# A hybrid state-space and DeltaNet trunk: branch products, gates and merge turned channel-major, and temporaries moved by 32 bytes

## The chip, the cores and the metric

The kernel runs on one core of a Trainium2 chip. The metric is the device time of one execution in microseconds (us), the median over the runs. The engines are named as in the profile: PE (TensorE, the matrix unit; PEld is its weight load), DVE (VectorE), ACT (ScalarE), POOL (GpSimd) and SP (SyncE, which issues the DMAs). A matmul multiplies a *stationary* operand of 128 x 128, loaded into the array, with a *moving* operand that streams through it. Sums are formed in PSUM, in banks of 128 partitions x 512 fp32 values; everything else lies in SBUF.

## The reference

256 tokens of width 1024 go through two layers. Each is a feed-forward half step, a mixer, and another half step. The mixer runs two branches on the same normalised input and merges them through two gates:

```python
for l in range(DEPTH):
    h = h + 0.5 * swiglu(rms_norm(h, ffn1_norm[l]), ffn1_w_in[l], ffn1_w_out[l])
    u = rms_norm(h, mix_norm[l])
    (z_s, xbc, dt_s, qkv, z_d, b_d, a_d, gate_s, gate_d) = jnp.split(u @ w_in[l], split_points, axis=-1)
    y_s = mamba2_branch(z_s, xbc, dt_s, ...)
    y_d = deltanet_branch(qkv, z_d, b_d, a_d, ...)
    merged = (jax.nn.sigmoid(gate_s) * (y_s @ ssm_w_branch[l])
              + jax.nn.sigmoid(gate_d) * (y_d @ dn_w_branch[l]))
    h = h + merged @ w_out[l]
    h = h + 0.5 * swiglu(rms_norm(h, ffn2_norm[l]), ffn2_w_in[l], ffn2_w_out[l])
return rms_norm(h, final_norm)
```

The change concerns `gate_s`, `gate_d`, the two branch products, the merge, and what feeds and follows them. The state-space branch is normalised in four groups: the last step of each group scales its result `yg` by `rsqrt(mean(yg*yg) + EPS)`.

## The kernel before

**Products.** Every large product is formed from two-part operands: a value x is split into xh (rounded to fp32r) and xl = x - xh, and a product is the three matmuls h·h, h·l and l·h. `mm3` (lines 208 to 211) holds the tokens stationary and moves 512 columns of weights; its result is token-major, 128 tokens x 512 channels in one bank. `mm3w` (213 to 216) holds weights stationary and moves 256 tokens; its result is channel-major, 128 channels x 256 tokens. In the profile the token-major products carry the names `t` (units of the input projection, the gates `tg` among them), `b` (branch products) and `o` (output products); channel-major ones are `fc` (feed-forward), `xs`, `kk`, `qq`, `vv`, `bc` and others. Rows of the profile name the split operands: `uTh`/`uTl` is the normalised input with channels on partitions, `bh`/`bl` the branch input, `mh`/`ml` the merged value, `whi`/`wlo` the weights.

**Weights.** They come in halves of 128 x 1024 through one DMA queue in the order in which they are used. ACT writes `whi` from a half (line 60) and DVE `wlo` (line 63), up to five halves ahead (`take`, `prep`, `load`).

**The mixer.** A table of unit names, `ORDER`, lists in which order the units of the mixer are written down. The tile scheduler makes from it one instruction stream for each engine; each engine runs its stream in order and waits on semaphores of the others. The merge is written with a raised priority. Units of interest:
- `xGi`: a piece of the state-space input of group G, `xs`, with its convolution `ca` on DVE.
- `DG`: the decay matrix `dc` of group G, among its steps a multiply `dc<-dc,cbt` over 128 x 2048 on DVE.
- `SG` and `TG`: first and second part of the state-space step of group G. `TG` ends with the group's norm: ACT sums squares into `sss` (`jk,sss<-yz`), DVE scales `sss` (line 71), POOL raises it to the power -1/2 (`srr`, line 119), and ACT scales two tiles of `yz` with it (`yz<-yz,srr`).
- `gSnp`: half p of gate S (0 for the state-space branch, 1 for DeltaNet), columns 512n. ACT applies tanh(x/2), and the merge forms (1 + tanh) times the branch result. (The factor one half is applied behind `w_out`, with the residual sum.)
- `o`, line 883: `dn_T(0)`, four transposes `oT` on PE, `og` on DVE, and the split of `og` into `bh` on ACT and `bl` on DVE: input of the first of four stages of the DeltaNet branch.
- `N`: the DeltaNet branch product (`dn_branch`, 929), four stages, and the product with its gate. It is followed by `y`, the first input of the state-space branch (`ss_T`, transposes `yT`).

After `ORDER` come the state-space branch (eight stages), the merge and the product with `w_out`. **Merge** (989 to 1003): for each 128 tokens and 512 channels, `mt` = (1 + gate) times branch, `tg` += `mt`, four transposes `mT` of 128 x 128 on PE, since `w_out` needs channels on partitions, then `mh` on ACT and `ml` on DVE.

**Pools.** `cpool`, `wpool` and `slots` hold lasting tiles. Behind them `s2` holds nine rotating temporaries of 128 x 512 (among them `bh`, `bl`, `og`, `mt`) and `sm` small ones. All tiles of `s2` begin at a multiple of 128 bytes of a partition. `uTh` and `uTl` begin 32 bytes behind one, `whi` and `wlo` at one.

Of the kernel before, what the change touches and what calls it, by code (L numbers as in the profile page):

```python
# [16 lines left out]
P = 128  # L17
# [19 lines left out]

ORDER = """
z20 s z10 z11 s z21 s M k1 k0 q1 k2 k3 K1 K0 q3 q0 K3 K2 v0 q2 I Q0 I Q3 I z30 v1 z31 Q2 v2 V0 I v3
V1 I V3 I Q1 V2 d0 R R R b3 R b2 b0 R b1 R d2 R x00 R d1 x01 R d3 R R P R g100 g101 D0 S0 x10 T0 D1  # L40
x11 g110 g111 S1 x20 T1 o x21 N D2 y S2 D3 x30 x31 T2 g000 g010 g001 S3 g011 T3
""".split()


# [1 line left out]
def trunk_kernel(ctx, tc, x, wst, wsm, norms, lpar, rpar, cst, out):  # L46
# [3 lines left out]
    cpool = ctx.enter_context(tc.tile_pool(name="cpool", bufs=1))  # L50
    wpool = ctx.enter_context(tc.tile_pool(name="wpool", bufs=1))
    slots = ctx.enter_context(tc.tile_pool(name="slots", bufs=1))
    s2 = ctx.enter_context(tc.tile_pool(name="s2", bufs=9))
    sm = ctx.enter_context(tc.tile_pool(name="sm", bufs=1))
    accp = ctx.enter_context(tc.tile_pool(name="accp", bufs=4, space=PSUM))
# [3 lines left out]
    def act(o, i, func=AF.Copy, **kw):  # L59
        return A.activation(out=o, in_=i, func=func, **kw)  # L60

    def tt(o, a, b, op):
        return V.tensor_tensor(out=o, in0=a, in1=b, op=op)  # L63

    def stt(o, a, s, b, op0, op1):
        return V.scalar_tensor_tensor(out=o, in0=a, scalar=s, in1=b, op0=op0, op1=op1)
# [6 lines left out]
    def f(ap):  # L73
        return ap.bitcast(F32)

    def tmp2(name):
        return s2.tile([P, 512], F32, tag="s2", name=name)

    def trb(name):
        return trp.tile([P, 512], F32, tag="tr", name=name)  # L80

    def accb(name):
        return accp.tile([P, 512], F32, tag="acc", name=name)
# [63 lines left out]
    LAST = cs[:, 6 * P : 7 * P]  # L147
    mhalf = cpool.tile([P, 1], F32, name="mhalf")
    V.memset(mhalf[:], -0.5)

    one = cpool.tile([1, P], F32, name="one")
    V.memset(one[:], 1.0)
# [57 lines left out]
        PE.matmul(ps, lh, rl, start=False, stop=False)  # L210
        PE.matmul(ps, ll, rh, start=False, stop=stop)  # L211

    def mm3w(ps, wh, wl, mh, ml, start, stop):
        PE.matmul(ps, wh, mh, start=start, stop=False)  # L214
        PE.matmul(ps, wh, ml, start=False, stop=False)  # L215
        PE.matmul(ps, wl, mh, start=False, stop=stop)  # L216

    def tok_chunk(ps, ks):

# [110 lines left out]
    def mixer(l, nxt):  # L330
# [20 lines left out]
        def tok_unit(key, part, done):  # L351

            if part != 1:
                open_[key] = [accb("t0"), accb("t1")]
            tok_chunk(open_[key], range(KT) if part is None else range(4 * part, 4 * part + 4))
            if part != 0:
                for t in range(2):
                    done(t, open_[key][t])
# [512 lines left out]

        tg = {}

        def gate(s_, n, part):
            if s_ not in tg:
                tg[s_] = slots.tile([P, 2, D], F32, tag=("sA", "sD")[s_], name="tg")
            v = tg[s_][:, :, n * 512 : (n + 1) * 512]
            tok_unit(("g", s_, n), part, lambda t, ps: act(v[:, t, :], ps[:], AF.Tanh, scale=0.5))


        brT = {}
# [26 lines left out]
                stt(ol[:, k], bank[:, k * S : (k + 1) * S], w, f(oh[:, k]), ALU.mult, ALU.subtract)  # L908
            brT[("s", j)] = (oh, ol)

        def branch(kind, n, mk, tail=1):
            ps = [[accb("b"), accb("b")] for _ in range(2)]
            held = {}

            def stat(k, t):
                oh, ol = held[k // 2]
                return oh[:, k % 2, t * P : (t + 1) * P], ol[:, k % 2, t * P : (t + 1) * P]

            made = 1
            for j0 in list(range(n - tail)) + [n - tail]:  # L920
                js = range(j0, j0 + (tail if j0 == n - tail else 1))
                while made < min(js[-1] + 2, n):
                    mk(made)
                    made += 1
                for j in js:
                    held[j] = brT.pop((kind, j))
                out_chunks(ps, stat, [2 * j + i for j in js for i in range(2)], 2 * n - 1, group=2 * len(js))
            return ps

        def dn_branch():  # L930
            ps = branch("d", 4, dn_T)
            m = tg[1]
            for t in range(2):
                for n in range(2):
                    sl = slice(n * 512, (n + 1) * 512)
                    stt(m[:, t, sl], m[:, t, sl], 1.0, ps[t][n][:], ALU.add, ALU.mult)

        sc, inv, rc = scalars(), invert(), recur()
        units = {"k": k_unit, "q": q_unit, "v": v_unit}
# [42 lines left out]

        for name in ORDER:
            step(name)
        m = tg[1]
        ps = branch("s", 8, ss_T)
        mh = slots.tile([P, KT, S], F32R, tag="sE", name="mh")
        ml = slots.tile([P, KT, S], F32R, tag="sH", name="ml")
        def merge(t):
            for n in range(2):  # L990
                sl = slice(n * 512, (n + 1) * 512)
                mt = tmp2("mt")
                stt(mt[:], tg[0][:, t, sl], 1.0, ps[t][n][:], ALU.add, ALU.mult)
                tt(m[:, t, sl], m[:, t, sl], mt[:], ALU.add)
                bank = trb("mT")
                for k in range(4):
                    PE.transpose(bank[:, k * P : (k + 1) * P], m[:, t, n * 512 + k * P : n * 512 + (k + 1) * P], ident)
                oh = mh[:, 4 * n : 4 * n + 4, t * P : (t + 1) * P]
                ol = ml[:, 4 * n : 4 * n + 4, t * P : (t + 1) * P]
                bv = bank[:].rearrange("p (k t) -> p k t", k=4)  # L1000
                act(oh, bv)
                tt(ol, bv, f(oh), ALU.subtract)

        for t in range(2):
            with tc.high_priority(offset=PRI):
                merge(t)
        po = [[accb("o"), accb("o")] for _ in range(2)]

        def stat(k, t):
# [23 lines left out]
def _layout(inp):  # L1033
# [21 lines left out]
    for l in range(DEPTH):  # L1055
        def ffn(wi, wo):
            gate, up = wi[:, :FF], wi[:, FF:]
            wst.append(cols(np.concatenate([gate[:, :256], up[:, :256]], axis=1)))
            both = np.stack([gate[:, 256:].reshape(D, -1, P), up[:, 256:].reshape(D, -1, P)], axis=2)
            wst.append(chans(both.reshape(D, -1)))  # L1060
            wst.append(rows(wo))

        ffn(inp["ffn1_w_in"][l], inp["ffn1_w_out"][l])
        w = inp["w_in"][l]
        o = 0
        parts = []
        for s in (2048, 3072, 32, 3072, 1024, 8, 8, 1024, 1024):
            parts.append(w[:, o : o + s])
            o += s
        z_s, xbc, dt_s, qkv, z_d, b_d, a_d, g_s, g_d = parts  # L1070
        zs, kc, qc, vc = cols(z_s), chans(qkv[:, 1024:2048]), chans(qkv[:, :1024]), chans(qkv[:, 2048:])
        xc, zd, gs, gd = chans(xbc[:, :2048]), chans(z_d), cols(g_s), cols(g_d)
        pieces = {"N": rows(inp["dn_w_branch"][l])}
        pieces.update({f"z{g}{i}": zs[2 * g + i : 2 * g + i + 1] for g in range(GS) for i in range(2)})
        for key, w, n in (("k", kc, 4), ("q", qc, 4), ("v", vc, 4), ("d", zd, 4), ("b", chans(xbc[:, 2048:]), 4)):
            pieces.update({f"{key}{i}": w[i : i + 1] for i in range(n)})
        pieces.update({f"x{g}{i}": xc[2 * g + i : 2 * g + i + 1] for g in range(GS) for i in range(2)})
        for s, w in enumerate((gs, gd)):
            pieces.update({f"g{s}{n}{i}": w[2 * n + i : 2 * n + i + 1] for n in range(2) for i in range(2)})
        wst += [zs[:2]] + [pieces[name] for name in ORDER if name in pieces]  # L1080
        wst.append(rows(inp["ssm_w_branch"][l]))
        wst.append(rows(inp["w_out"][l]))
        ffn(inp["ffn2_w_in"][l], inp["ffn2_w_out"][l])
        wsm.append(np.concatenate([dt_s, a_d, b_d], axis=1).reshape(KT, P, 48).transpose(1, 0, 2))
        cw = np.zeros((48, P, 5), f32)
        dc = inp["dn_conv_w"][l]
        sc = inp["ssm_conv_w"][l]
        sb = inp["ssm_conv_b"][l]
        order = [(dc, 1024, 8, None), (dc, 0, 8, None), (dc, 2048, 8, None), (sc, 2048, 8, sb), (sc, 0, 16, sb)]
        i = 0  # L1090
        for cwt, c0, n, bias in order:
            for j in range(n):
                sl = slice(c0 + j * P, c0 + (j + 1) * P)
                cw[i, :, :4] = cwt[:, sl].T
                if bias is not None:
                    cw[i, :, 4] = bias[sl]
                i += 1
        lpar.append(
            np.concatenate(
                [cw.transpose(1, 0, 2).reshape(P, 240), inp["ssm_norm"][l].reshape(16, P).T, inp["dn_norm"][l].reshape(P, 1)],  # L1100
                axis=1,
            )
        )
        rpar.append(
            np.concatenate(
                [inp["ssm_dt_bias"][l], inp["dn_dt_bias"][l], inp["ssm_a_log"][l], inp["dn_a_log"][l], inp["ssm_d"][l]]
            )
        )
        norms += [inp["ffn1_norm"][l], inp["mix_norm"][l], inp["ffn2_norm"][l]]
# [40 lines left out]
```

## Time and profile before

| | us |
|---|---|
| median of three runs | 1596.07 |
| lowest and highest run | 1594.54 and 1596.31 |
| the profiled execution | 1593.43 |
| its span in the profile | 1591.6 |
| PE busy in the span | 1572.3 |
| DVE busy | 1069.1 |
| ACT busy | 880.1 |
| POOL busy | 58.1 |

Rows of the timeline give the start of an instruction and its duration, both in us, the engine, the line, the operation and its tile (out<-in), the shapes and a count. In square brackets stands how long the engine was idle before it, and what ended that. Rows of groups end with the busy time in us, the mean in ns of one instruction, and the idle time before them. Rows of windows give the stretch, its length, the busy time with the number of instructions that it touches, the granted TensorE clock (1.00 is full), the DMA share and GB/s. Matmuls overlap in the array: the listed duration of one is longer than the distance from its start to that of the next.

### The profile page before, as it was taken

Reading aid. Unit: us, or ns where it says so; the run is one execution under the profiler, and the core shown is the slowest. Engines: PE = TensorE matmul, PEld = TensorE weight load, DVE = VectorE, ACT = ScalarE, POOL = GpSimd, SP = SyncE. Lnnn points to the kernel's source line nnn. Section 1 sums busy time; section 2 is a strip of 40 time slices with the busy share of each in tenths; the row PEclk is TensorE's granted clock in tenths of the full one; section 3 lists DMA queues with packets and bytes.
Section 4 is the critical chain, followed back from the end, with each engine's and each line's share of the span. In section 5 each row is a group of like instructions: output and inputs, shape, how many; then the busy total and the mean of one; then the engine's idle time right before and its main releaser. Section 6 shows DMA issues by size and latency. Waiting matters only on the chain.

```text
span 1591.6 us, 28859 instructions
## 1 busy us (share of the span) xinstructions
PE 1572.3 (99%) x11672; PEld 1420.9 (89%) x11672; DVE 1069.1 (67%) x1550; ACT 880.1 (55%) x1416; POOL 58.1 (4%) x60
## 2 busy tenths in 40 slices
PE   8999999999999999999999999999999999999998
PEld 7999879999888888999899987899998888889986
DVE  5555468957899766555465555698579996675554
ACT  5444468756565654444354444686656665454443
POOL 0000020000000000000000001000000000000000
PEclk9999999999999999999999999999999999999999
DMA  7555465543465456555565565655436555555562
GB/s 268 193 188 195 161 203 192 166 149 117 173 214 172 159 170 189 188 192 190 173 207 190 186 196 174 197 176 180 129 120 207 178 170 175 172 175 194 187 196 96
DMA packets 91915, 284.73 MB, mean 179 GB/s; under 512 B 22069, under 2 KB 23045, under 8 KB 90758
## 3 DMA queue, kind: packets, MB, share of 16 engines
q1 hardware_dynamic: 91782, 282.90, 54.8%
q8 instruction: 91, 1.49, 0.4%
q14 instruction: 42, 0.34, 0.1%
HBM read 280.94 MB, written 1.92 MB: 178 GB/s over the span
## 4 chain that ended last, share of the span: by engine, by line
PE 91%; DVE 4%; DMA 2%; ACT 1%; POOL 1%; issue 0%; SPq 0%; POOLq 0%; ACTq 0%
PE fc L216 9%; PE fc L214 9%; PE fc L215 9%; PE o L211 6%; PE o L209 5%; PE o L210 5%; PE t L209 4%; PE t L210 3%; PE t L211 3%; PE b L211 3%; PE b L210 2%; PE b L209 2%; PE xs L215 2%; PE xs L214 2%; PE xs L216 2%; DVE wlo L63 1%
## 5 line engine op out<-in xcount | busy, mean ns | idle before, releaser
L63 DVE TENSOR_TENSOR wlo<-wraw,whi 128x1024 fp32r<-128x1024 f32 x504 | 613.6, 1223 | 376.4 <-ACT whi L60 369.3
L60 ACT ACTIVATE whi<-wraw 128x1024 fp32r<-128x1024 f32 x504 | 531.0, 1060 | 429.3 <-PE fc L215 176.2
L214 PE MATMUL fc<-uTh,whi 128*128 128x256 f32 x1280 | 357.4, 279 | 0.0
L215 PE MATMUL fc<-uTl,whi 128*128 128x256 f32 x1280 | 357.0, 279 | 0.0
L216 PE MATMUL fc<-uTh,wlo 128*128 128x256 f32 x1280 | 357.0, 279 | 0.0
L215 PEld LDWEIGHTS fc<-uTl,whi 128*128 128x128 f32 x1280 | 240.6, 188 | 0.2
L214 PEld LDWEIGHTS fc<-uTh,whi 128*128 128x128 f32 x1280 | 240.6, 188 | 0.2
L216 PEld LDWEIGHTS fc<-uTh,wlo 128*128 128x128 f32 x1280 | 240.6, 188 | 0.0
L209 PE MATMUL o<-whi,gh 128*128 128x512 f32 x352 | 137.3, 390 | 0.0
L210 PE MATMUL o<-wlo,gh 128*128 128x512 f32 x352 | 137.3, 390 | 0.0
L211 PE MATMUL o<-whi,gl 128*128 128x512 f32 x352 | 137.0, 389 | 0.0
L209 PE MATMUL t<-whi,uTh 128*128 128x512 f32 x256 | 103.2, 404 | 1.0 <-ACT uTh L60 1.0
L210 PE MATMUL t<-wlo,uTh 128*128 128x512 f32 x256 | 101.6, 397 | 0.0
L211 PE MATMUL t<-whi,uTl 128*128 128x512 f32 x256 | 101.1, 396 | 0.0
L211 PEld LDWEIGHTS o<-whi,gl 128*128 128x128 f32 x352 | 66.1, 188 | 13.8
L210 PEld LDWEIGHTS o<-wlo,gh 128*128 128x128 f32 x352 | 66.1, 188 | 13.6
L209 PEld LDWEIGHTS o<-whi,gh 128*128 128x128 f32 x352 | 66.1, 188 | 13.4
L209 PE MATMUL b<-whi,bh 128*128 128x512 f32 x192 | 76.3, 399 | 0.0
L210 PE MATMUL b<-wlo,bh 128*128 128x512 f32 x192 | 74.9, 390 | 0.0
L211 PE MATMUL b<-whi,bl 128*128 128x512 f32 x192 | 74.3, 394 | 0.6 <-DVE bl L63 0.6
L214 PE MATMUL xs<-uTh,whi 128*128 128x256 f32 x256 | 73.1, 286 | 0.0
L216 PE MATMUL xs<-uTh,wlo 128*128 128x256 f32 x256 | 71.6, 280 | 0.0
(259 smaller groups left out, 2915.6 us busy)
## 6 DMA issues: line engine op xcount, KB each, us to landing
wraw<-in_wst_dram SPq DMA_DIRECT2D x504, 512.0 KB, 4.3
dc<-rdram SPq DMA_DIRECT2D x8, 1024.0 KB, 9.2
nw<-in_norms_dram SPq DMA_DIRECT2D x6, 512.0 KB, 4.9
gb<-rdram SPq DMA_DIRECT2D x8, 256.0 KB, 6.1
h<-in_x_dram SPq DMA_DIRECT2D x4, 256.0 KB, 3.1
out_dram<-fo SPq DMA_DIRECT2D x4, 256.0 KB, 2.3
dq<-X SPq DMA_DIRECT2D x2, 256.0 KB, 4.8
cs<-in_cst_dram SPq DMA_DIRECT2D x1, 384.0 KB, 8.2
```

The source lines that it names most:

```text
L60: return A.activation(out=o, in_=i, func=func, **kw)
L63: return V.tensor_tensor(out=o, in0=a, in1=b, op=op)
L209: PE.matmul(ps, lh, rh, start=start, stop=False)
L210: PE.matmul(ps, lh, rl, start=False, stop=False)
L211: PE.matmul(ps, ll, rh, start=False, stop=stop)
L214: PE.matmul(ps, wh, mh, start=start, stop=False)
L215: PE.matmul(ps, wh, ml, start=False, stop=False)
L216: PE.matmul(ps, wl, mh, start=False, stop=stop)
```

## The change

Three parts:
1. Gates and branch products are formed channel-major: weights stationary, 256 tokens moving. A gate unit is now two channel groups of 128 in one bank, so four units `gS0` to `gS3` per gate in place of two pairs. In a branch each of the four banks holds two channel groups and takes its products stage by stage. The gate weights come in another layout, cut by channels.
2. The merge works on these channel-major tiles: gate, sum, `mh`, `ml`, without transposes and without the temporary `mt`.
3. A new pool `shift` with a tile of 32 bytes stands ahead of `s2` and `sm`, so that all their tiles begin 32 bytes behind a multiple of 128. POOL sets that tile to zero once.

```diff
-x11 g110 g111 S1 x20 T1 o x21 N D2 y S2 D3 x30 x31 T2 g000 g010 g001 S3 g011 T3
+x11 g12 g13 S1 x20 T1 o x21 N D2 y S2 D3 x30 x31 T2 g00 g01 g02 S3 g03 T3
...
+    shift = ctx.enter_context(tc.tile_pool(name="shift", bufs=1))
     s2 = ctx.enter_context(tc.tile_pool(name="s2", bufs=9))
     sm = ctx.enter_context(tc.tile_pool(name="sm", bufs=1))
...
+    gap = shift.tile([P, 8], F32, name="gap")
+    G.memset(gap[:], 0.0)
...
-        def gate(s_, n, part):
+        def gate(s_, u):
+
             if s_ not in tg:
-                tg[s_] = slots.tile([P, 2, D], F32, tag=("sA", "sD")[s_], name="tg")
-            v = tg[s_][:, :, n * 512 : (n + 1) * 512]
-            tok_unit(("g", s_, n), part, lambda t, ps: act(v[:, t, :], ps[:], AF.Tanh, scale=0.5))
+                tg[s_] = slots.tile([P, KT, S], F32, tag=("sA", "sD")[s_], name="tg")
+            ps = accb("g")
+            chan_chunk(ps)
+            act(tg[s_][:, 2 * u : 2 * u + 2, :].rearrange("p k t -> p (k t)"), ps[:], AF.Tanh, scale=0.5)
...
+        def branch(kind, n, mk):
+
+            ps = [accb("b") for _ in range(4)]
+            mk_at = 1
+            for j in range(n):
+                while mk_at < min(j + 2, n):
+                    mk(mk_at)
+                    mk_at += 1
+                oh, ol = brT.pop((kind, j))
+                ws = [take(), take()]
+                for b in range(4):
+                    for k, (wh, wl) in enumerate(ws):
+                        for a in range(2):
+                            c0 = (2 * b + a) * P
+                            mm3w(
+                                ps[b][:, a * S : (a + 1) * S], wh[:, c0 : c0 + P], wl[:, c0 : c0 + P],
+                                oh[:, k], ol[:, k], j == 0 and k == 0 and a == 0, j == n - 1 and k == 1, True,
+                            )
             return ps
+
+        def pair(v, b):
+
+            return v[:, 2 * b : 2 * b + 2, :].rearrange("p k t -> p (k t)")
...
-        def merge(t):
-            for n in range(2):
-                sl = slice(n * 512, (n + 1) * 512)
-                mt = tmp2("mt")
-                stt(mt[:], tg[0][:, t, sl], 1.0, ps[t][n][:], ALU.add, ALU.mult)
-                tt(m[:, t, sl], m[:, t, sl], mt[:], ALU.add)
-                bank = trb("mT")
-                for k in range(4):
-                    PE.transpose(bank[:, k * P : (k + 1) * P], m[:, t, n * 512 + k * P : n * 512 + (k + 1) * P], ident)
-                oh = mh[:, 4 * n : 4 * n + 4, t * P : (t + 1) * P]
-                ol = ml[:, 4 * n : 4 * n + 4, t * P : (t + 1) * P]
-                bv = bank[:].rearrange("p (k t) -> p k t", k=4)
-                act(oh, bv)
-                tt(ol, bv, f(oh), ALU.subtract)
+        with tc.high_priority(offset=PRI):
+            for b in range(4):
+                g, m = pair(tg[0], b), pair(tg[1], b)
+                stt(g, g, 1.0, ps[b][:], ALU.add, ALU.mult)
+                tt(m, m, g, ALU.add)
+                act(pair(mh, b), m)
+                tt(pair(ml, b), m, f(pair(mh, b)), ALU.subtract)
```

The scheduler makes other streams from this. Three places are of interest; the first two look the same in both layers. Line numbers of the changed kernel are shifted by a few.

ACT ahead of the DeltaNet branch `N` of the first layer, before: `jk,sss` are the sums of squares that end the second group's `T1`, `bh<-og` is the input of the first branch stage.

```order
L60 ACTIVATE jk,sss<-yz 128x512
L60 ACTIVATE whi<-wraw 128x1024
L60 ACTIVATE jk,sss<-yz 128x512
L60 ACTIVATE ca<-xs,lp 128x256
L60 ACTIVATE bh<-og 128x512
L60 ACTIVATE xsT<-ca 128x256
L60 ACTIVATE yz<-yz,srr 128x512 x2
L60 ACTIVATE whi<-wraw 128x1024
L60 ACTIVATE bh<-og 128x512
```

The same place in the changed kernel:

```order
L61 ACTIVATE jk,sss<-yz 128x512
L61 ACTIVATE whi<-wraw 128x1024
L61 ACTIVATE ca<-xs,lp 128x256
L61 ACTIVATE jk,sss<-yz 128x512
L61 ACTIVATE whi<-wraw 128x1024
L61 ACTIVATE xsT<-ca 128x256
L61 ACTIVATE yz<-yz,srr 128x512 x2
L61 ACTIVATE bh<-og 128x512 x2
```

The first `bh<-og` stood ahead of the pair `yz<-yz,srr` and stands behind it now, next to the second.

DVE at the start of the second part of group 1, `T1`, in the first layer, before: `xdt` and `xe` are inputs of its matmuls, `xD` the first result, and `sss` follows fifteen rows below the first row of `dc`.

```order
L63 TENSOR_TENSOR xe<-xdt,dE 128x512
L63 TENSOR_TENSOR wlo<-wraw,whi 128x1024
L70 TENSOR_SCALAR dc<-dc 128x2048
L66 SCALAR_TENSOR_TENSOR ca<-xs,lp,ca 128x255
L63 TENSOR_TENSOR xD<-xD,ydb 128x512
```

The same place in the changed kernel:

```order
L64 TENSOR_TENSOR xe<-xdt,dE 128x512
L64 TENSOR_TENSOR wlo<-wraw,whi 128x1024
L64 TENSOR_TENSOR dc<-dc,cbt 128x2048
L67 SCALAR_TENSOR_TENSOR ca<-xs,lp,ca 128x255
L64 TENSOR_TENSOR xD<-xD,ydb 128x512
```

The scaling `dc<-dc` of the third group has moved some eight rows up, and its multiply `dc<-dc,cbt`, which stood eleven rows behind `sss`, now stands ahead of it: of all instructions that DVE runs up to this `sss`, it is the only one more.

PE from the state-space branch to `w_out` of the first layer, before:

```order
L210 MATMUL b<-wlo,bh 128x512
L997 MATMUL mT<-cs,tg 128x128 x8
L211 MATMUL b<-whi,bl 128x512
L209 MATMUL b<-whi,bh 128x512
L210 MATMUL b<-wlo,bh 128x512
L211 MATMUL b<-whi,bl 128x512
L209 MATMUL o<-whi,mh 128x512
```

The same place in the changed kernel:

```order
L218 MATMUL b<-bh,whi 128x256
L219 MATMUL b<-bl,whi 128x256
L220 MATMUL b<-bh,wlo 128x256
L212 MATMUL o<-whi,mh 128x512
L213 MATMUL o<-wlo,mh 128x512
L212 MATMUL o<-whi,mh 128x512
L213 MATMUL o<-wlo,mh 128x512
L214 MATMUL o<-whi,ml 128x512
```

The transposes are gone (two more groups of four stood further on among the products of `w_out`), and `w_out` begins with four products that use `mh` alone.

More of the change, by code (lines that the diff above doesn't have):

```diff
@@ L39 @@
 z20 s z10 z11 s z21 s M k1 k0 q1 k2 k3 K1 K0 q3 q0 K3 K2 v0 q2 I Q0 I Q3 I z30 v1 z31 Q2 v2 V0 I v3
-V1 I V3 I Q1 V2 d0 R R R b3 R b2 b0 R b1 R d2 R x00 R d1 x01 R d3 R R P R g100 g101 D0 S0 x10 T0 D1
-x11 g110 g111 S1 x20 T1 o x21 N D2 y S2 D3 x30 x31 T2 g000 g010 g001 S3 g011 T3
+V1 I V3 I Q1 V2 d0 R R R b3 R b2 b0 R b1 R d2 R x00 R d1 x01 R d3 R R P R g10 g11 D0 S0 x10 T0 D1
+x11 g12 g13 S1 x20 T1 o x21 N D2 y S2 D3 x30 x31 T2 g00 g01 g02 S3 g03 T3
 """.split()
@@ L211, in mm3, with mm3w @@
         PE.matmul(ps, ll, rh, start=False, stop=stop)
[L213 to L216, printed above, removed]
+    def mm3w(ps, wh, wl, mh, ml, start, stop, shared=False):
+        PE.matmul(ps, wh, mh, start=start, stop=False, skip_group_check=shared)
+        PE.matmul(ps, wh, ml, start=False, stop=False, skip_group_check=shared)
+        PE.matmul(ps, wl, mh, start=False, stop=stop, skip_group_check=shared)
     def tok_chunk(ps, ks):
@@ L909, in ss_T @@
             brT[("s", j)] = (oh, ol)
[L911 to L927, printed above, removed]
-            return ps
+        def branch(kind, n, mk):
[15 more added lines that the diff above has]
+                            )
+            return ps
+        def pair(v, b):
+            return v[:, 2 * b : 2 * b + 2, :].rearrange("p k t -> p (k t)")
         def dn_branch():
             ps = branch("d", 4, dn_T)
-            m = tg[1]
-            for t in range(2):
-                for n in range(2):
-                    sl = slice(n * 512, (n + 1) * 512)
-                    stt(m[:, t, sl], m[:, t, sl], 1.0, ps[t][n][:], ALU.add, ALU.mult)
+            for b in range(4):
+                v = pair(tg[1], b)
+                stt(v, v, 1.0, ps[b][:], ALU.add, ALU.mult)
         sc, inv, rc = scalars(), invert(), recur()
@@ L984, in mixer @@
             step(name)
-        m = tg[1]
         ps = branch("s", 8, ss_T)
@@ L988, in mixer @@
         ml = slots.tile([P, KT, S], F32R, tag="sH", name="ml")
-        def merge(t):
-            for n in range(2):
-                sl = slice(n * 512, (n + 1) * 512)
-                mt = tmp2("mt")
-                stt(mt[:], tg[0][:, t, sl], 1.0, ps[t][n][:], ALU.add, ALU.mult)
-                tt(m[:, t, sl], m[:, t, sl], mt[:], ALU.add)
-                bank = trb("mT")
-                for k in range(4):
-                    PE.transpose(bank[:, k * P : (k + 1) * P], m[:, t, n * 512 + k * P : n * 512 + (k + 1) * P], ident)
-                oh = mh[:, 4 * n : 4 * n + 4, t * P : (t + 1) * P]
-                ol = ml[:, 4 * n : 4 * n + 4, t * P : (t + 1) * P]
-                bv = bank[:].rearrange("p (k t) -> p k t", k=4)
-                act(oh, bv)
-                tt(ol, bv, f(oh), ALU.subtract)
-        for t in range(2):
-            with tc.high_priority(offset=PRI):
-                merge(t)
+        with tc.high_priority(offset=PRI):
+            for b in range(4):
+                g, m = pair(tg[0], b), pair(tg[1], b)
[3 more added lines that the diff above has]
+                tt(pair(ml, b), m, f(pair(mh, b)), ALU.subtract)
         po = [[accb("o"), accb("o")] for _ in range(2)]
@@ L1071, in _layout @@
         zs, kc, qc, vc = cols(z_s), chans(qkv[:, 1024:2048]), chans(qkv[:, :1024]), chans(qkv[:, 2048:])
-        xc, zd, gs, gd = chans(xbc[:, :2048]), chans(z_d), cols(g_s), cols(g_d)
+        xc, zd, gs, gd = chans(xbc[:, :2048]), chans(z_d), chans(g_s), chans(g_d)
         pieces = {"N": rows(inp["dn_w_branch"][l])}
@@ L1078, in _layout @@
         for s, w in enumerate((gs, gd)):
-            pieces.update({f"g{s}{n}{i}": w[2 * n + i : 2 * n + i + 1] for n in range(2) for i in range(2)})
+            pieces.update({f"g{s}{i}": w[i : i + 1] for i in range(4)})
         wst += [zs[:2]] + [pieces[name] for name in ORDER if name in pieces]
```

## The prediction

> **What bounds the kernel now.** I read the page's busy times and clock first, then its chain of waits, then the groups by line, and last the timelines of the places that the change touches.
>
> ```profile
> span 1591.6 us, 28859 instructions
> PE 1572.3 (99%) x11672; PEld 1420.9 (89%) x11672; DVE 1069.1 (67%) x1550; ACT 880.1 (55%) x1416; POOL 58.1 (4%) x60
> PEclk9999999999999999999999999999999999999999
> PE 91%; DVE 4%; DMA 2%; ACT 1%; POOL 1%; issue 0%; SPq 0%; POOLq 0%; ACTq 0%
> L209 PE MATMUL b<-whi,bh 128*128 128x512 f32 x192 | 76.3, 399 | 0.0
> ```
>
> TensorE (PE) is busy for 99% of the span at full clock and carries 91% of the chain. So the change can win or lose only in the starts of PE: by the pitch of its matmuls, by matmuls that fall away, and by new waits. The last row counts the branch products: 192 of each of the three terms of a product, 576 matmuls in the program's two layers.
>
> **Pitch.** Matmuls overlap, so the price of one is the distance between starts, not its listed duration.
>
> ```profile
> 434.08 0.28 PE L214 MATMUL xs<-uTh,whi 128*128 128x256 f32 x1
> ...
> 438.98 0.28 PE L214 MATMUL xs<-uTh,whi 128*128 128x256 f32 x1
> 449.41 0.40 PE L209 MATMUL t<-whi,uTh 128*128 128x512 f32 x1
> ...
> 458.51 0.40 PE L209 MATMUL t<-whi,uTh 128*128 128x512 f32 x1
> 579.10 0.39 PE L209 MATMUL b<-whi,bh 128*128 128x512 f32 x1
> ...
> 586.58 0.39 PE L209 MATMUL b<-whi,bh 128*128 128x512 f32 x1
> ```
>
> 42 starts lie between the first two rows, 39 between the next, 33 between the last: 4.90/42 = 0.1167 us for 256 columns with a weight tile stationary, 9.10/39 = 0.2333 for 512 columns in the token-major units `t` (gates among them), 7.48/33 = 0.2267 in the branch `b`.
>
> Gates: each 512-column matmul becomes two of 256, 2 x 0.1167 = 0.2333. That is the old price, so 0. Each layer's eight tanh on ACT stay eight of 128x512.
>
> Branches: 576 x 0.2267 = 130.6 us become 1152 x 0.1167 = 134.4, **+3.8 us**. The nearest row, `xs`, is the same form as the new branch: weights stationary, and a moving tile (`uTh`) that already lies 32 bytes behind a multiple of 128, as `bh` will. What another placing of the moving tile would cost no row shows; the bound below is half of the old pitch, 0.1133, which gives 0. I take the row.
>
> The Trainium skill ("TensorE: Matmul & The Clock Gate", Back-to-back issue gap) gives an isolated matmul N/2.4 + 2.5 ns, 109 at 256 columns and 216 at 512; as an estimate by that page the term would be +1.5. Both of its figures lie under the pitches here (117 and 227), so the measurement decides.
>
> **The merge.** Before, 16 transposes `mT` per layer stand in the stream of PE.
>
> ```profile
> 586.81 0.39 PE L210 MATMUL b<-wlo,bh 128*128 128x512 f32 x1
> 587.04 1.21 PE L997 MATMUL mT<-cs,tg 128*128 128x128 f32 x8
> 588.01 0.48 PE L211 MATMUL b<-whi,bl 128*128 128x512 f32 x1
> ...
> 590.40 0.50 PE L211 MATMUL o<-whi,ml 128*128 128x512 f32 x1 [0.32 <-DVE ml L63]
> 586.81:593.94 7.13, 6.81 (x38) 1.00 0.44 144
> 590.86 0.68 DVE L66 SCALAR_TENSOR_TENSOR mt<-tg,b 128x512 f32<-128x512 f32 x1
> 591.46 0.68 DVE L63 TENSOR_TENSOR ml<-mT,mh 128x512 fp32r<-128x512 f32 x1
> ```
>
> The window from 586.81 to 593.94 touches 38 matmuls: one that is running at its start, one that begins at its end, 16 transposes and 20 products (4.53 us at 0.2267). The remaining 2.60 are the transposes, 0.97 for the first eight by the starts around them and so near 1.7 for all (two later groups of four cost 0.35 each in the same view), and some 0.9 of waits and restarts. All of it goes if the new seam does not wait. In the new branch the last stage works bank by bank, 12 matmuls each, so the four banks end 4.2, 2.8, 1.4 and 0 us ahead of the end of the branch, and merging begins while PE still multiplies. Per bank VectorE (DVE) does three instructions at 0.60 us pitch (590.86 to 591.46) and ACT one; behind the last two `wlo` of the branch I get bank 0's `mh` 0.75 us before and its `ml` 0.4 us after the branch's end. The first four products of `w_out` need `mh` alone (0.9 us). The last `ml` is there at +5.6, and the last quarter of 96 products at 0.2267 begins at +16. So nothing waits: 2 x 2.60 = **-5.2 us**. If the seam waited as long as before (0.9) it would be -3.3.
>
> **The new wait.** Two instructions are moved, both shown row by row ahead of this text. On DVE the `dc<-dc,cbt` of the third state-space group now stands ahead of the second group's rest, which ends in `sss`; on ACT the first `bh<-og` of the DeltaNet branch now stands behind the two `yz<-yz,srr`, which wait for POOL's power, which waits for `sss`. Before, that `bh` went first:
>
> ```profile
> 475.70 0.15 DVE L71 TENSOR_SCALAR sss<-sss 128x2 f32<-128x2 f32 x1
> 475.93 2.21 POOL L119 TENSOR_TENSOR srr<-sss,mhalf 128x2 f32<-128x2 f32 x1 [25.62 <-DVE sss L71]
> 475.76 0.62 ACT L60 ACTIVATE bh<-og 128x512 fp32r<-128x512 f32 x1
> 478.17 1.34 ACT L60 ACTIVATE yz<-yz,srr 128x512 f32<-128x512 f32 x2 [1.49 <-POOL srr L119]
> 479.41 1.05 ACT L60 ACTIVATE whi<-wraw 128x1024 fp32r<-128x1024 f32 x1
> 476.43:483.10 6.67, 6.37 (x25) 1.00 0.33 95
> 476.34 0.27 PE L902 MATMUL yT<-cs,yz 128*128 128x128 f32 x1
> 476.43 0.50 PE L209 MATMUL b<-whi,bh 128*128 128x512 f32 x1
> 482.76 0.50 PE L211 MATMUL b<-whi,bl 128*128 128x512 f32 x1 [0.30 <-DVE bl L63]
> 483.10 0.39 PE L209 MATMUL b<-whi,bh 128*128 128x512 f32 x1
> ```
>
> PE reached the branch at 476.43, the moment `bh` ended. In the new order it arrives there as early, and behind the branch's first matmul stands all of PE. When does `bh` end now?
>
> ```profile
> 445.88 2.28 DVE L63 TENSOR_TENSOR dc<-dc,cbt 128x2048 f32<-128x2048 f32 x1
> 448.08 0.47 DVE L66 SCALAR_TENSOR_TENSOR ca<-xs,lp,ca 128x255 f32<-128x255 f32 x1
> 441.10:475.70 34.60, 33.88 (x50) 1.00 0.67 222
> L119 POOL TENSOR_TENSOR srr<-sss,mhalf x8: 697/1604/2205, 448.7 to 1331.3; 128x2 f32<-128x2 f32 x8
> 482.02 0.68 DVE L63 TENSOR_TENSOR bl<-og,bh 128x512 fp32r<-128x512 f32 x1
> ```
>
> The moved multiply takes 448.08 - 445.88 = 2.20 us of DVE. The window shows DVE busy for 33.88 of 34.60 us ahead of `sss`, so at most 0.72 is absorbed: `sss` comes 1.5 to 2.2 late, at 477.2 to 477.9; I take 477.55. POOL starts 0.23 later (as 475.70 to 475.93) and takes 0.70 to 2.21, median 1.60: the end is 479.38. The two `yz` take 1.24 on ACT (478.17 to 479.41), `bh` 0.62: 481.27, the first product at 481.32. The new order lets three products pass before `bl`, which DVE has ready 0.68 later; PE runs freely from about 482.07. With the same work before (three half products, 0.35, and three transposes `yT` at the 0.09 between 476.34 and 476.43) the old kernel stood at 477.05: 5.02 late, with a restart of 0.11 (482.76 to 483.10 against 0.2267) 5.13. Against this stand the old kernel's own waits on the same stretch, which the new order of chunks lacks: the window of PE's branch products from 476.43 to 483.10 counts 25, so 24 pitches (5.44) and two `yT` (0.18) in 6.67 us, 1.05 of waits. Net 4.08, say **+4.1 us per layer**, +8.2 in two; the second layer's rows read alike. PE is the bound after it as before it, so no later slack gives it back.
>
> Bounds: with DVE not late at all and POOL's shortest 0.70 it is 4.1 - 1.85 - 0.90 = 1.35; with `sss` at 477.9 and 2.21 it is 5.1.
>
> **Small parts.** POOL's one memset runs at the start on an engine busy 58 us. ACT and DVE write tiles 32 bytes off at no price that a row shows:
>
> ```profile
> L63 DVE TENSOR_TENSOR uTl<-hnT,uTh 128x512 fp32r<-128x512 f32 x24 | 15.7, 686 | 5.8 <-ACT uTh L60 5.7
> L63 DVE TENSOR_TENSOR ml<-mT,mh 128x512 fp32r<-128x512 f32 x8 | 5.5, 684 | 0.1
> ```
>
> `uTl` lies at 32, `ml` at 0: 686 against 684 ns. As stationary operand a tile at 32 (`t`) costs 6.7 ns more than one at 0 (`b`); some 144 transposes of temporaries get such an operand, up to 1 us, much of it behind waits. I take 0.
>
> **Sum.** -5.2 + 3.8 + 8.2 = **+6.8 us**. The profiled execution took 1593.43 (its span 1591.6 and 1.8 around it), so 1600.2 is expected; the runs have a median of 1596.07, 2.6 more, and on that scale it is **1602.9**.
>
> **The rivals.**
> - *The chain is short* (not slower). DVE gives up idle time and `sss` comes no later, POOL's power takes its 0.70, and the wait is 1.35 per layer: -5.2 + 3.8 + 2.7 = +1.3, 1597.4. For it: POOL takes 0.70 in two of its eight, and what follows `sss` on DVE has changed. Against it: DVE's 0.72 of idle time. It decides from a wait under (3.2 + 1.4) / 2 = 2.3 per layer: `bl` ready before about 480.3.
> - *The wait lowers the clock.* PE would stand from about 476.8 to 481.3, 4.5 us. The longest PE wait inside the mixer is 1.6, with the granted clock at 1.00:
>
> ```profile
> PE cbb L778 <- DVE vb L63: 2.0, 2, 1.6
> 12.36 0.63 PE L209 MATMUL f<-whi,uTh 128*128 128x512 f32 x1
> 14.50 0.63 PE L211 MATMUL f<-whi,uTl 128*128 128x512 f32 x1
> ```
>
> At the program's start, behind idle time, five pitches take 2.14: 0.43 each instead of 0.2333. If each wait were followed by ten 512-column pitches of that kind, 2 us per layer are added: +10.8, 1606.9. No trace here holds a pause so long in mid-program. The Trainium skill (same page, HAM oscillation) states the rule: no PE gap over about 3.4 us, or the clock halves until the array has been busy again. With windows that run freely a pause of 4.5 need not cover one, so I hold it under an even chance.
> - *The aligned pitch.* If the new branch runs at 0.1133, its term is 0 and the sum +3.0: 1599.1, still slower through the wait.
> - *No late `bh`.* If ACT's order did not bind, -5.2 + 3.8 = -1.4, 1594.7. The rows `whi` behind `yz` at 479.41 show that ACT keeps its order, so this is slight.
>
> **Chances.** Forecast 0.57; clock 0.18; short chain 0.12; aligned pitch 0.08; no late `bh` 0.05. Under 0.2% (3.2 us) a measurement cannot tell this kernel from no change. The last case and the short chain give "same" and, with the aligned pitch, a little "faster": faster 0.06, same 0.18, slower 0.76. The range reaches from 1596.5 (a short chain with part of the cheaper pitch) to 1608 (wait at its upper bound, 1604.9, with part of the clock's loss).
>
> **What would show it.** The first `b` after the `oT` transposes should start about 4.7 us behind the last `yT`, with a wait on ACT's `bh`, in both layers; ACT should idle on `srr` with `bh` right behind; `sss` should stand 1.5 to 2.2 us later against PE; branch rows should have a pitch of 0.1167; from the branch's last matmul to `w_out`'s no pitch should exceed 0.25. I am wrong if `bh` is ready before PE, if the granted clock leaves 1.00, or if the seam waits for `mh`.

## The result, and the profile after

The changed kernel takes 1602.57 us, the median of four runs (1601.62 to 1603.47), beside 1595.3 for the kernel before in the same comparison: a ratio of 1.0048 with an interval of 1.0031 to 1.0066, so 4.9 to 10.5 us slower. Forecast were 1602.9 and 6.8 us more.

The page of the changed kernel, its busy times, the clock, and the branch's first term; then PE's waits (us in total, times, the longest):

```profile
span 1600.5 us, 30716 instructions
PE 1576.5 (99%) x12600; PEld 1469.0 (92%) x12600; DVE 1068.0 (67%) x1550; ACT 878.0 (55%) x1416; POOL 55.1 (3%) x61
PEclk9999999999999999999999999999999999999999
L218 PE MATMUL b<-bh,whi 128*128 128x256 f32 x384 | 108.7, 288 | 6.8 <-ACT bh L61 6.8
```

```profile
PE b L218 <- ACT bh L61: 6.8, 2, 3.4
```

PE is the bound as before, and one new row leads its waits: twice 3.4 us for the first `bh` of the DeltaNet branch, once in each layer. The page's slices of 40 us show no lower clock, since a fall of a few microseconds leaves each of them over nine tenths. The timeline of the place in the first layer, PE:

```profile
475.68 0.66 PE L908 MATMUL yT<-cs,yz 128*128 128x128 f32 x4
479.72 0.61 PE L218 MATMUL b<-bh,whi 128*128 128x256 f32 x3 [3.38 <-ACT bh L61]
480.45 0.39 PE L219 MATMUL b<-bl,whi 128*128 128x256 f32 x1
...
481.12 0.42 PE L220 MATMUL b<-bh,wlo 128*128 128x256 f32 x1
481.33 0.41 PE L218 MATMUL b<-bh,whi 128*128 128x256 f32 x1
481.55 0.41 PE L219 MATMUL b<-bl,whi 128*128 128x256 f32 x1
...
484.32 0.28 PE L218 MATMUL b<-bh,whi 128*128 128x256 f32 x1
484.43 0.28 PE L219 MATMUL b<-bl,whi 128*128 128x256 f32 x1
```

The windows of PE around it (stretch, length, busy, granted clock):

```profile
480.45:484.32 3.87, 3.87 (x20) 0.56 0.27 104
484.32:490.00 5.68, 5.68 (x50) 1.00 0.00 0
1270.45:1276.20 5.75, 5.75 (x26) 0.50 0.28 92
```

After the wait the clock is granted at 0.56 for 3.87 us: the products start 0.21 us apart (481.12, 481.33, 481.55) where 0.1167 is the pitch at full clock, from 484.32 on. The last row is the second layer, where PE starts again at 1270.45: there the clock is at half for 5.75 us. What PE waited for, on DVE, POOL and ACT:

```profile
475.95 0.15 DVE L72 TENSOR_SCALAR sss<-sss 128x2 f32<-128x2 f32 x1
476.01 1.21 DVE L64 TENSOR_TENSOR wlo<-wraw,whi 128x1024 fp32r<-128x1024 f32 x1
476.17 1.61 POOL L120 TENSOR_TENSOR srr<-sss,mhalf 128x2 f32<-128x2 f32 x1 [24.78 <-DVE sss L72]
477.81 1.33 ACT L61 ACTIVATE yz<-yz,srr 128x512 f32<-128x512 f32 x2 [1.03 <-POOL srr L120]
479.06 0.61 ACT L61 ACTIVATE bh<-og 128x512 fp32r<-128x512 f32 x1
```

The chain is the forecast one: `sss`, POOL's power, two scalings on ACT, and only then `bh`, whose end at 479.67 releases PE.

### The profile page after: what moved, and what is told of

It reads as the page before. It is cut to its first block, busy times and chain, and to the rows that moved or that the text cites. A ratio compares the mean times of both kernels' runs of the same rounds, so it can differ in the third digit from the quotient of the medians.

```text
span 1600.5 us, 30716 instructions
## 1 busy us (share of the span) xinstructions
PE 1576.5 (99%) x12600; PEld 1469.0 (92%) x12600; DVE 1068.0 (67%) x1550; ACT 878.0 (55%) x1416; POOL 55.1 (3%) x61
## 4 chain that ended last, share of the span: by engine, by line
PE 91%; DVE 4%; DMA 2%; ACT 1%; POOL 1%; issue 0%; SPq 0%; POOLq 0%; DVEq 0%; ACTq 0%
PE fc L218 9%; PE fc L219 9%; PE fc L220 9%; PE o L214 5%; PE o L212 5%; PE o L213 5%; PE b L219 3%; PE b L220 3%; PE b L218 3%; PE g L218 2%; PE g L220 2%; PE g L219 2%; PE t L212 2%; PE t L213 2%; PE t L214 2%; PE xs L218 1%
## 5 line engine op out<-in xcount | busy, mean ns | idle before, releaser
L218 PE MATMUL b<-bh,whi 128*128 128x256 f32 x384 | 108.7, 288 | 6.8 <-ACT bh L61 6.8
L219 PE MATMUL b<-bl,whi 128*128 128x256 f32 x384 | 109.2, 285 | 0.1
L220 PE MATMUL b<-bh,wlo 128*128 128x256 f32 x384 | 108.7, 284 | 0.0
L218 PEld LDWEIGHTS b<-bh,whi 128*128 128x128 f32 x384 | 73.3, 193 | 7.2 <-ACT bh L61 7.2
L219 PEld LDWEIGHTS b<-bl,whi 128*128 128x128 f32 x384 | 74.2, 193 | 0.3 <-DVE bl L64 0.3
L220 PEld LDWEIGHTS b<-bh,wlo 128*128 128x128 f32 x384 | 74.2, 193 | 0.0
L218 PE MATMUL g<-uTh,whi 128*128 128x256 f32 x256 | 73.0, 285 | 0.0
```

The source lines that it names most:

```text
L218: PE.matmul(ps, wh, mh, start=start, stop=False, skip_group_check=shared)
L219: PE.matmul(ps, wh, ml, start=False, stop=False, skip_group_check=shared)
L220: PE.matmul(ps, wl, mh, start=False, stop=stop, skip_group_check=shared)
```

## The experiments

All were timed in five rounds or more beside the kernel before. For the stages there is also a measure within one execution: the time from the start of PE's last `cbb` row to that of its last `o<-whi,mh` row in a layer, the mixer's second half. In both layers, in us:

| kernel | median | ratio to before, interval | second half, layer 1 and 2 |
|---|---|---|---|
| before | 1595.07 to 1595.52 | | 190.52, 190.55 |
| `after_again`, the change again | 1602.75 | 1.0049, 1.0035 to 1.0063 | 194.52, 194.88 |
| `o_early` | 1590.24 | 0.9968, 0.9955 to 0.998 | 189.03, 188.98 |
| `keepwarm` | 1600.23 | 1.0032, 1.002 to 1.0045 | 193.57, 193.58 |
| `noshift` | 1605.41 | 1.0059, 1.0046 to 1.0072 | 196.27, 196.28 |
| `before_gap` | 1598.32 | 1.0015, 1.0004 to 1.0026 | 193.93, 192.78 |
| `before_late` | 1601.44 | 1.003, 1.0019 to 1.0041 | 193.67, 193.97 |
| `cbt_back` | 1594.41 | 0.999, 0.998 to 1.0001 | 190.85, 190.55 |
| `cbt_back_late` | 1600.16 | 1.0026, 1.0017 to 1.0035 | 194.16, 193.22 |
| `x30_fill` | 1594.56 | 0.999, 0.9979 to 1.0 | 190.55, 190.38 |
| `o_early_cbt` | 1589.86 | 0.9963, 0.9949 to 0.9976 | 189.11, 189.09 |

### The change again, and `bh` early

> The changed kernel as it is, for a scale beside the others. Theory A (the late bh costs a wait of 3.4 us and the clock's fall behind it another 1.7 to 2 us per layer; pitch +3.8 and seam -5.2 in all): +7 us against before, TensorE waits for ACT's bh twice 3.4 us, and the granted clock is about 0.55 for 4 us behind each wait. Rival B (the clock's fall was an accident of one execution): +3 to +4 us, granted clock 1.00 there.

Measured: 7.7 us slower than before, and the wait and the low clock in both layers again. Theory A.

```diff
-x11 g12 g13 S1 x20 T1 o x21 N D2 y S2 D3 x30 x31 T2 g00 g01 g02 S3 g03 T3
+x11 g12 g13 S1 x20 o T1 x21 N D2 y S2 D3 x30 x31 T2 g00 g01 g02 S3 g03 T3
```

> The first DeltaNet branch input is written ahead of T1, so that its bh stands ahead of the two scalings of yz on ACT again; all else as in the change. Theory A: both waits and both falls of the clock go, at least 4.6 us per layer: 1.4 to 2 us faster than before the change (ratio about 0.999), 9 us faster than the changed kernel. Rival C (the wait only moves to the second branch stage, whose bh still stands behind the scalings): the wait of TensorE for bh comes back there with 2 us or more per layer, and the time is 1598 or more. Rival D (the loss lies in the 256-column branch itself): still 5 us or more slower than before.

Measured: 1590.24, 12.5 us faster than the change and 4.8 us faster than before (3.2 to 7.2 by the interval). The moved word `o` takes the whole unit with it, its four transposes, `og` and `bl` too. On ACT `bh` now ends nine microseconds ahead of the scalings, and PE passes from the transposes straight into the branch; the window covers the whole DeltaNet branch.

```profile
466.79 0.63 ACT L61 ACTIVATE bh<-og 128x512 fp32r<-128x512 f32 x1 [0.23 <-DVE og L67]
476.37 1.34 ACT L61 ACTIVATE yz<-yz,srr 128x512 f32<-128x512 f32 x2 [0.20 <-POOL srr L120]
477.61 0.62 ACT L61 ACTIVATE bh<-og 128x512 fp32r<-128x512 f32 x1
```

```profile
474.08 0.60 PE L893 MATMUL oT<-cs,vb 128*128 128x128 f32 x4
474.44 0.37 PE L218 MATMUL b<-bh,whi 128*128 128x256 f32 x1
```

```profile
474.44:497.72 23.28, 23.28 (x203) 1.00 0.53 166
```

PE is busy for 23.28 of 23.28 us at full clock, though the second `bh` still stands behind the scalings: it is ready (477.61 + 0.62) before its stage begins. Rivals C and D fall. What the change cost beyond its gains is the late `bh`, 5.5 to 5.9 us in each layer by the table. This kernel is faster than both.

### The clock's share

```diff
                 ws = [take(), take()]
+                if kind == "d" and j == 0:
+                    fill = trb("fill")
+                    for i in range(12):
+                        PE.matmul(fill[:], uTh[:, i % KT, :P], ws[0][0][:, :512], start=i == 0, stop=i == 11)
                 for b in range(4):
```

> The changed kernel with twelve unread 512-column products (2.8 us) on TensorE in each layer's pause ahead of the DeltaNet branch; the late bh stays. Theory A: TensorE begins the branch as late as in the changed kernel, but the granted clock stays 1.00: 3.4 to 4 us faster than the changed kernel in two layers, still 3 us slower than before. Rival B' (the slow pitch of 0.21 us has to do with the first products of the branch, its banks or its operands, not with the pause): no faster than the changed kernel, the slow rows stay.

```profile
474.50 3.04 PE L930 MATMUL fill<-whi,uTh 128*128 128x512 f32 x12
477.37 1.04 PE L893 MATMUL oT<-cs,vb 128*128 128x128 f32 x8
479.77 0.62 PE L218 MATMUL b<-bh,whi 128*128 128x256 f32 x3 [1.04 <-ACT bh L61]
480.50 0.39 PE L219 MATMUL b<-bl,whi 128*128 128x256 f32 x1
```

```profile
479.77:484.00 4.23, 4.23 (x34) 1.00 0.46 144
```

The branch begins as late as in the change (479.77 against 479.72) and with 12 idle products more, but the clock stays at 1.00, and the kernel is 2.5 us faster, 1.0 to 1.3 per layer by the table. That is theory A's direction and less than its 3.4 to 4. So the pause, not the first products, lowers the clock. By the change's own rows the slow stretch of the first layer holds 19 pitches in 3.87 us (480.45 to 484.32), 2.22 at full clock, so it costs 1.65 us. In `after_again` the clock is low from the first product of the branch on (0.50 from 479.18 to 482.50). There the slow clock costs less, since PE waits for `bl` anyhow: its first product starts 0.81 us behind the branch's first in `after_again` and 0.73 in `keepwarm`. The idle products also push eight transposes back by 2.9 us, but not the next `og` (480.75 against 480.70).

### The same wait in the kernel before

In `before_late` an ordering, without any work, holds the first `bh<-og` behind the last scaling of group 1.

```diff
-                act(yv, yv, scale=rr[:, t : t + 1])
+                state["yz"] = act(yv, yv, scale=rr[:, t : t + 1])
...
-            act(oh[:].rearrange("p a t -> p (a t)"), og[:])
+            with ExitStack() as st:
+                if hp == 0:
+                    st.enter_context(tc.issue_after(state["yz"].ins))
+                act(oh[:].rearrange("p a t -> p (a t)"), og[:])
```

> The kernel before, token-major as it was, with the first bh of the DeltaNet branch ordered behind the two scalings of yz on ACT (the DVE's order left as it is). Theory A (the late bh alone makes the loss, whatever the layout): TensorE waits 3 us or more per layer for bh, the clock may fall behind it; +5 to +9 us against before. Rival D (only the 256-column branch suffers): within 2 us of before.

```profile
476.70 0.60 PE L905 MATMUL yT<-cs,yz 128*128 128x128 f32 x4
479.83 0.80 PE L209 MATMUL b<-whi,bh 128*128 128x512 f32 x1 [2.54 <-ACT bh L60]
480.43 0.63 PE L210 MATMUL b<-wlo,bh 128*128 128x512 f32 x1
480.86 0.63 PE L209 MATMUL b<-whi,bh 128*128 128x512 f32 x1
```

```profile
479.83:483.50 3.67, 3.67 (x10) 0.59 0.48 156
```

Measured: 6.0 us slower, 3.2 to 3.4 per layer, so rival D falls: token-major products suffer a wait and a low clock too (a pitch of 0.43). The loss is smaller than the 5.5 to 5.9 us per layer in the change. The wait is 2.54, under the 3 us expected: `sss` (at 476.05) stands ahead of the transposes `yT` here as in the kernel before.

### DVE's part

The multiply alone is put back behind `sss`, for group 2:

```diff
-            tt(dc[:], dc[:], late["cbm"][:, g, None].to_broadcast([P, 8, 2, P]), ALU.mult)
+            with ExitStack() as st:
+                if g == 2:
+                    st.enter_context(tc.issue_after(state["sss", 1].ins))
+                tt(dc[:], dc[:], late["cbm"][:, g, None].to_broadcast([P, 8, 2, P]), ALU.mult)
```

> The changed kernel with the third group's dc<-dc,cbt ordered behind the second group's sss on DVE, and nothing else asked for; the scheduler then puts the first bh ahead of the scalings of yz on ACT by itself. bl stands behind that multiply (2.2 us) on DVE now. Theory A: no wait on bh; a short one on bl (2.2 us less what the three products ahead of it cover, up to 1.8 per layer), clock 1.00; so 4 to 8 us faster than the changed kernel, 1593 to 1598.

Measured: 1594.41, 8.3 us faster than the change, no wait on `bh`, clock at 1.00. The short wait on `bl` is there, 0.2 us in each layer where up to 1.8 was expected:

```profile
PE b L219 <- DVE bl L64: 0.4, 2, 0.2
```

The kernel stays 4.2 us behind `o_early`, 1.6 to 1.8 per layer by the table. In this order `bh` precedes the scalings without being asked to, so the place of the multiply is enough to turn the order on ACT. Why the scheduler does so was not looked into; presumably it expects `sss` at another time.

`cbt_back_late` adds the ordering of `before_late` to it, so that DVE's part is undone and ACT's is kept:

> As the run before, with the first bh nevertheless held behind the scalings of yz: DVE's part undone, ACT's part left. Theory A (sss was about 1 us late through the moved multiply, the rest of the wait is the chain itself): TensorE waits about 2 to 2.6 us for bh instead of 3.4; with bl's place some more; if the pause stays under what lowers the clock, the slow rows go: 1597 to 1600. Rival H (the multiply's move is all of the wait): wait under 0.5 us.

Measured: PE waits 2.4 to 2.5 us for `bh` instead of 3.4, so undoing the multiply's move takes 0.9 to 1.0 off the wait, and rival H falls. But the clock falls here too, as the window behind the wait shows, and the kernel gains only 2.6 us on the change:

```profile
479.13 0.62 PE L218 MATMUL b<-bh,whi 128*128 128x256 f32 x3 [2.42 <-ACT bh L61]
479.13:483.00 3.87, 3.77 (x18) 0.60 0.26 70
```

With `bh` early, the multiply's place should be worth nothing; `o_early_cbt` has both edits:

> The run with bh early and besides the third group's dc<-dc,cbt back behind sss on DVE. Theory A: TensorE waits nowhere in the branch with bh early alone, so the multiply's place is worth nothing by itself: within 1 us of that run, 1590. Rival H (the multiply's move costs by itself): 2 us faster than it.

Measured: 1589.86 and 189.1 per layer, as `o_early` (1590.24 and 189.0).

### Another cover for the wait

```diff
-x11 g12 g13 S1 x20 T1 o x21 N D2 y S2 D3 x30 x31 T2 g00 g01 g02 S3 g03 T3
+x11 g12 g13 S1 x20 T1 o x21 x30 N D2 y S2 D3 x31 T2 g00 g01 g02 S3 g03 T3
```

> The changed kernel with one state-space input unit (x30, 48 products of 256 columns, 5.6 us) moved ahead of the DeltaNet branch; the first bh stays behind the scalings of yz on ACT. Theory A (only TensorE's standing costs, not the late bh as such): no wait for bh over 0.5 us, granted clock 1.00, as fast as the run with bh early: 1589 to 1592. Rival I (the moved unit brings its own waits: its conversion and convolution work on ACT and DVE stands ahead of the branch's inputs): 1593 or more.

Measured: 1594.56, 8.2 us faster than the change but 4.3 slower than with `bh` early, so theory A's time is missed and rival I's is met. The wait for the first `bh` is gone and the clock stays up; two short waits remain in the branch, which the waits of PE name (for the second `bh` and for a `ca`):

```profile
PE b L218 <- ACT bh L61: 0.8, 2, 0.4
PE b L218 <- DVE ca L67: 0.3, 2, 0.2
```

On ACT two `whi`, an `xsT` and two `ca` stand between the first `bh` (480.11) and the second (484.62). From start to start the places of these two waits, and that of the first `bl`, take 0.65, 0.43 and 0.41 us in the first layer, where some 0.12 is usual: 1.1 of the 1.5 us by which the second half of the layer is longer than in `o_early`. The rest was not followed up.

### The 32 bytes

`noshift` leaves out the tile and its pool in the changed kernel, `before_gap` adds both to the kernel before.

> The changed kernel without the 32-byte tile, so that bh and bl begin at multiples of 128 again. Theory A (the offset of a moving tile does not set the pitch of 256 columns): branch pitch 0.1167 as with the shift, time within 1 us of the changed kernel. Rival E (an unshifted moving tile is cheaper): 0.1133, 3.8 us faster. Rival F (an unshifted moving tile is dearer, which is what the shift is for): pitch over 0.12, each 0.01 us costs 11.5 us.

Rows of the state-space branch, 51 starts apart in `noshift`, then 30 apart in the change:

```profile
588.82 0.28 PE L216 MATMUL b<-bl,whi 128*128 128x256 f32 x1
...
594.94 0.28 PE L216 MATMUL b<-bl,whi 128*128 128x256 f32 x1
```

```profile
589.94 0.28 PE L218 MATMUL b<-bh,whi 128*128 128x256 f32 x1
...
593.44 0.28 PE L218 MATMUL b<-bh,whi 128*128 128x256 f32 x1
```

6.12/51 = 0.1200 without the shift, 3.50/30 = 0.1167 with it. Theory A is wrong: the pitch changes with the offset of the moving tile, in the direction of rival F, by 3.3 ns. Over 1152 products that is 3.8 us; the runs show 2.7 (1605.41 against 1602.75).

> The kernel before with the 32-byte tile alone: bh and bl, which are stationary operands there, begin 32 bytes off. Theory A (a stationary operand 32 bytes off costs 6.7 ns per 512-column product, as t against b showed): the branch pitch rises from 0.2267 to 0.2333, 576 products, +3.8 us. Rival G (the pitch of t has to do with its units, not with the offset): branch pitch stays 0.2267, time within 1 us of before.

```profile
582.83 0.40 PE L214 MATMUL b<-whi,bl 128*128 128x512 f32 x1
...
591.93 0.40 PE L214 MATMUL b<-whi,bl 128*128 128x512 f32 x1
```

9.10/39 = 0.2333 against 0.2267: theory A. Stationary, the same tiles lose by the shift; the kernel is 2.9 us slower (0.6 to 4.1). Its profiled execution, the slowest of the twelve, also holds pauses of 3.1 and 2.0 us at `cbb`, one in each layer, with a low clock behind each, so its row of the table says less.

## Why the prediction was right

The time came out as forecast, +7.3 us against +6.8, and so did its cause, a late `bh` on the forecast chain. But that the sum is so near is luck: a wait sized too long and a loss of clock put at nothing went against each other. One of the signs that the prediction named for being wrong came true, since the granted clock left 1.00.

**The pitch: right.** Gates and branches run at 0.1167, and the branch's rise came as forecast: a stage of the state-space branch starts 6.04 us after the one before (546.18 to 552.22), 5.91 before the change (541.43 to 547.34), 0.13 more and 0.16 forecast.

**The seam: right but for a tenth.** From the branch into `w_out`:

```profile
593.67 0.28 PE L220 MATMUL b<-bh,wlo 128*128 128x256 f32 x1
593.79 0.39 PE L212 MATMUL o<-whi,mh 128*128 128x512 f32 x1
...
594.48 0.40 PE L213 MATMUL o<-wlo,mh 128*128 128x512 f32 x1
594.73 0.50 PE L214 MATMUL o<-whi,ml 128*128 128x512 f32 x1
595.07 0.40 PE L212 MATMUL o<-whi,mh 128*128 128x512 f32 x1
```

`mh` is there, and the first `ml` holds PE up by 0.13 us (0.25 and 0.34 instead of 0.2267 twice), where no pitch over 0.25 was forecast. Pitch, seam and the old kernel's waits of 1.05 were forecast at +1.9 - 2.6 - 1.05 = -1.75 per layer; `o_early`, which has these three and no late `bh`, shows -1.5.

**The late `bh`: the right place and chain, but a wait sized too long.** From `sss` to the end of `bh` the forecast was 477.55 to 481.27, 3.72 us; measured 475.95 to 479.67, 3.72 (POOL's power, which could take 0.70 to 2.21, took 1.61). What failed is the step "`sss` comes 1.5 to 2.2 late". Against the first transpose `yT` ahead of the branch it stood 0.64 ahead before (475.70 and 476.34) and 0.27 behind now (475.95 and 475.68): 0.91. Counted from the last `cbb` of a layer, in both layers alike, `sss` came 1.31 later than before the change (54.18 and 52.87 us in the first), a little less than forecast, and PE's `yT` 0.40 later (53.91 and 53.51): PE came later too, which the working left out. It moved `sss` and held PE still. So PE stood for 3.4 us, where the working had 4.5 (476.8 to 481.3). `before_late` bears this out: with `sss` 0.65 ahead of `yT` (476.05 and 476.70) its wait is 2.54, 0.84 less. `cbt_back_late` comes to a like wait, 2.42, by another sum: `sss` is 1.82 ahead (474.29 and 476.11), but POOL's power takes 2.67 beside the multiply.

**The clock: a rival that came true beside the forecast.** It was priced at 2 us per layer and held at a chance of 0.18; the rows of the change show 1.65 in the first layer and at most 2.9 in the second (half of 5.75). The clock fell in both layers of all five executions that were profiled with the late `bh` and PE idle (granted 0.50 to 0.68 over the four microseconds behind the wait). The forecast sum without it was +6.8, measured +7.3: about 1 us per layer too much wait, and the whole loss of the clock too little. The working put the rival's time at 1606.9, on top of a wait that was itself too long.

**The short chain and the aligned pitch: wrong.** POOL took 1.61, not 0.70, and an unshifted moving tile is dearer, not cheaper. An estimate by the Trainium skill's formula ("TensorE: Matmul & The Clock Gate", Back-to-back issue gap) would have made the branch term +1.5; the rows agree with the measured pitch of `xs`, +3.8.

## What to carry to other kernels

When a change touches a scheduled kernel, compare the order of every engine first: here one input behind two scalings on ACT, with a multiply moved on DVE, cost 5.5 to 5.9 us per layer, more than all transposes removed, and one word moved in the table of units took that cost away, to 4.8 us under the kernel before. On the bound engine a pause can cost more than its length, when the clock falls behind it. When the cause can't be moved, useful work in the pause was worth more here than idle products (8.2 and 2.5 us). And when a transfer of lateness is worked out, ask whether the waiting engine comes later too.

## What the runs showed of the hardware

**A pause of 2 us can be enough for the clock, and one of 2.9 need not be.** The Trainium skill ("TensorE: Matmul & The Clock Gate", HAM oscillation) says that gaps over about 3.4 us make it fall. Here a shorter one was enough: in `before_late` the clock fell behind a wait of 2.54 us (0.59 behind it), and in the same execution not behind one of 2.87 at `cbb`:

```profile
422.66 0.70 PE L778 MATMUL cbb<-BC 128*128 128x256 f32 x2 [2.87 <-DVE vb L63]
```

```profile
422.66:426.00 3.34, 3.34 (x16) 1.00 0.03 12
```

In `before_gap`, at the same `cbb` and behind the same rows of PE, a wait of 2.01 in the second layer was enough:

```profile
1214.86 1.22 PE L781 MATMUL cbb<-BC 128*128 128x256 f32 x2 [2.01 <-DVE vb L64]
1214.86:1218.27 3.41, 3.41 (x9) 0.50 0.05 22
```

So neither the length of the pause nor the work ahead of it decides alone; whether it is the place of the pause in time stays open. Nor does the fall come in every execution: of the twelve runs of `before_late` five have a mean granted clock of 0.999, as the kernel before has in most of its runs, and seven have 0.996 to 0.998 (3.4 us at half clock in 1600 are 0.001). With the 3.4 us wait, all nine runs of the change have 0.995 to 0.997.

**POOL's power ends behind the TENSOR_TENSOR that DVE runs beside it.** Its 0.70, 1.60 and 2.21 us go with what DVE runs meanwhile. In `cbt_back` the 2.28 us multiply follows `sss`:

```profile
474.41 2.28 DVE L64 TENSOR_TENSOR dc<-dc,cbt 128x2048 f32<-128x2048 f32 x1
```

```profile
474.58 2.67 POOL L120 TENSOR_TENSOR srr<-sss,mhalf 128x2 f32<-128x2 f32 x1 [22.48 <-DVE sss L72]
```

It ends at 477.25, 0.56 after that multiply (476.69). In the change it ends at 477.78, 0.56 after `wlo` (477.22), and before the change at 478.14, 0.56 after the end of the `bl` of 476.90 (477.58). Beside the SCALAR_TENSOR_TENSOR `bl<-yT,lp,bh`, at 545.41 before the change, it took 0.70. The Trainium skill ("SBUF — State Buffer", Who interferes with whom) calls the port pair that DVE and POOL share an exclusive lock; these ends agree with it for the TENSOR_TENSOR rows.

**The price of 32 bytes has a sign.** A moving tile of 256 columns gains by it (0.1167 against 0.1200 us), a stationary one under 512 columns loses (0.2333 against 0.2267), with the other operand at a multiple of 128 in each case. Other offsets, and why it is so, were not tried.
